# A larger ring of weight tiles in the expert stage: thirteen instead of ten, with the expert inputs kept once in float32 and split tiles of half the size

## The chip, the cores and the metric

The kernel runs on one core of a Trainium2 chip. The metric is the device time of one execution in microseconds (us); three executions of the kernel before give a median of 1507.25 us (1500.32 to 1512.21).

## The reference, cut to what matters

A two-layer transformer trunk, one sequence of 256 tokens, width 1024, all in float32. Everything up to the last feed-forward block stands in the same order in both kernels. The block that the change is about is the mixture of experts at the end:

```python
def moe_swiglu(u, w_router, wg, wu, wd):            # u: 256 tokens x 1024
    logits = (xf @ w_router).astype(F32)            # 8 experts
    vals, idx = lax.top_k(logits, TOP_K_EXPERTS)    # 2 of them for each token
    w = jax.nn.softmax(vals, axis=-1)
    gate = jnp.sum(jax.nn.one_hot(idx, N_EXPERTS, dtype=F32) * w[..., None], axis=1)
    for e in range(N_EXPERTS):                      # wg, wu: 1024 x 3584, wd: 3584 x 1024
        y = y + gate[:, e:e + 1].astype(xf.dtype) * swiglu(xf, wg[e], wu[e], wd[e])
```

`u` is the normalized and modulated residual, and `swiglu(u, wg, wu, wd)` is `(silu(u @ wg) * (u @ wu)) @ wd`. The weights of the eight experts are 352 MB in float32, and each is read once.

## The kernel before, in words

**Experts by load.** A router ranks the experts by the number of tokens they got. The four fullest are "heavy" and get 128 token slots, the other four are "light" and get 64 (`SLOTS`). They are worked in turns, heavy, light, heavy, light (`ORDER`). A pair is one heavy and one light expert.

**Two ways to multiply.** For a heavy expert every weight is split into a high and a low float32r part, and each product is three matmuls: high by high, low by high, high by low (`mm3`, L379 to L382). ScalarE (ACT) writes the high part (a cast, L319), VectorE (DVE) subtracts it from the weight (L323). When the split has to be held back, it goes through L321 and L325, which add a zero made from what is waited for (`hold`, `wait`). For a light expert TensorE (PE) reads the raw float32 weights without a split (L1242, L1340); two 64-column halves of the array run at a time, and one float32 matmul of the source is two instructions on PE.

**Stages of an expert.** The hidden width of 3584 is taken in two parts, `CHS` = 2048 and 1536 columns ("first part", "second part"). For each part: the gate matrix in 8 tiles (`chunks_up`), then the silu of the result on ACT (`gated_of`, L1414/L1416), then half of the down matrix of the part before (`chunks_down`, `half(0)`), then the up matrix in 8 tiles, then the product of the two on DVE (`hidden_of`, L1426/L1428), then the other half of the down matrix of the part before (`half(1)`). So after the first part of a heavy expert's gate or up matrix come down tiles of the light expert before it (none for the first expert), and after its second part come its own down tiles.

**The gather.** `pick` builds a 0/1 matrix `P` (tokens by slots) and multiplies the normalized tokens with it on PE (L1188). The tokens are kept as `xh` (high part) and `xl` (low part), both float32r, 2 tiles of 128 x 1024 each. `low()` computes `xl` on DVE (L1050) after the router's choice; the first held splits wait for it.

**The ring.** Weights land in tiles of 128 x 2048 float32 (8 KB a partition, 1 MB). The first 13 tiles of the expert stage come from a list `once`; after it, `ring` hands out ten buffers in turn (eight of pool `raw`, two of `raw2`). SyncE (SP) issues all loads in order (L1215 for gate and up, L1320 for down), each when its buffer's last reader is done.

**The split tiles.** Pool `hl` has four `wh` and four `wl` tiles of 128 x 1024 each. `run` keeps up to three pieces of work prepared ahead of the one that PE uses (`AHEAD = 2`): for a heavy expert a piece is 1024 columns (six matmuls; 512 columns at the end of the second part), for a light one a whole tile.

```python
AHEAD = 2
...
while ready <= AHEAD:
    item = next(work, None)
    ...
    prepare, use = item
    queue.append((use, prepare and prepare(), prepare is not None))
    ready += prepare is not None
```

A scheduler in the tile framework sets the order of instructions on each engine; each engine runs its own list in order.

## Time and profile before

| | us |
|---|---|
| median of 3 executions | 1507.25 |
| lowest, highest | 1500.32, 1512.21 |
| the profiled execution | 1512.12 |
| its span, first to last instruction | 1509.8 |

The profile was taken from one execution. A line such as L323 is a line of the kernel before. "Busy" is the time in which an engine had an instruction running; instructions of one engine overlap at their ends, so a step from one start to the next is shorter than a duration. PEclk is the clock that the chip granted to TensorE, 1.00 being 2.4 GHz and 0.50 being 1.2 GHz. "Idle before" names the time for which an engine stood still and what ended that.

### The profile page before, as it was taken

How to read it: one execution, taken by the hardware profiler on the slowest of the kernel's cores; microseconds unless marked ns; L12 is line 12 of the kernel's file. 1: busy time of each engine (PE TensorE's matmuls, PEld its weight loads, DVE VectorE, ACT ScalarE, POOL GpSimd, SP SyncE). 2: the span in 40 equal slices, each digit the busy share in tenths (PEclk: the TensorE clock that was granted, in tenths of full speed). 3: DMA queues.
4: the chain of work that ended last, by engine and by line, in shares of the span. 5: the costliest groups of instructions: out<-in, count | busy, mean ns of one | idle time of the engine just before them, and what ended most of it. 6: DMA issues, size and time to landing. Idle time of an engine off the chain costs nothing. (4 is left out here: it accounts for less than half of the span.)

```text
span 1509.8 us, 19315 instructions
## 1 busy us (share of the span) xinstructions
PE 1436.0 (95%) x6845; PEld 945.7 (63%) x6845; DVE 940.2 (62%) x1552; ACT 704.5 (47%) x1102; POOL 6.3 (0%) x31
## 2 busy tenths in 40 slices
PE   6999899999999998999999999999999999999995
PEld 3764678888677547788554767445767445676541
DVE  3875599887778654899342778433677334686412
ACT  3536443434444554777223656323665314574311
POOL 0000000000000000000000000000000000000000
PEclk9999999999999969899999999999999999999998
DMA  9846679995767004669999999999999999999995
GB/s 340 325 156 230 257 277 364 365 332 198 243 231 260 40 1 168 209 241 381 405 369 396 421 405 403 368 408 408 420 374 411 367 401 420 419 362 422 391 419 217
DMA packets 118093, 484.01 MB, mean 321 GB/s; under 512 B 10410, under 2 KB 20836, under 8 KB 87268
## 3 DMA queue, kind: packets, MB, share of 16 engines
q1 hardware_dynamic: 117616, 482.60, 82.9%
q8 instruction: 56, 0.92, 0.2%
q14 instruction: 49, 0.40, 0.1%
q10 hardware_dynamic: 372, 0.10, 0.0%
HBM read 481.61 MB, written 1.05 MB: 320 GB/s over the span
## 5 line engine op out<-in xcount | busy, mean ns | idle before, releaser
L323 DVE TENSOR_TENSOR wl<-raw,wh 128x1024 fp32r<-128x1024 f32 (+1 forms) x468 | 515.2, 1138 | 114.3 <-ACT wh L319 105.2
L319 ACT CAST wh<-raw 128x1024 fp32r<-128x1024 f32 (+2 forms) x477 | 455.3, 985 | 267.3 <-PE mm L381 166.2
L1242 PE MATMUL mm<-raw,xr 128*64 128x512 f32 (+1 forms) x1024 | 206.3, 545 | 0.0
L380 PE MATMUL mm<-wh,e 128*128 128x512 f32 x448 | 178.5, 399 | 2.9 <-ACT wh L319 2.9
L381 PE MATMUL mm<-wh,e 128*128 128x512 f32 x448 | 177.2, 396 | 0.0
L380 PE MATMUL mm<-wh,uh 128*128 128x512 f32 (+4 forms) x432 | 163.5, 382 | 4.0 <-ACT wh L319 3.3
L381 PE MATMUL mm<-wh,ul 128*128 128x512 f32 (+4 forms) x432 | 163.6, 379 | 2.2 <-DVE ul L345 2.2
L382 PE MATMUL mm<-wl,uh 128*128 128x512 f32 (+4 forms) x432 | 160.9, 377 | 2.3 <-DVE wl L325 2.0
L382 PE MATMUL mm<-wl,e 128*128 128x512 f32 x448 | 151.4, 401 | 0.0
L1242 PEld LDWEIGHTS mm<-raw,xr 128*64 128x64 f32 x1024 | 68.2, 136 | 110.7 <-issue 102.1
L1340 PE MATMUL y<-raw,lh 128*64 128x512 f32 x448 | 108.6, 599 | 3.3 <-DMA raw<-in_moe_w_down 2.2
L380 PEld LDWEIGHTS mm<-wh,e 128*128 128x128 f32 x448 | 85.5, 191 | 23.8 <-ACT wh L319 6.1
L382 PEld LDWEIGHTS mm<-wl,e 128*128 128x128 f32 x448 | 84.7, 191 | 24.7 <-DVE wl L323 2.7
L381 PEld LDWEIGHTS mm<-wh,e 128*128 128x128 f32 x448 | 85.3, 190 | 17.4
L380 PEld LDWEIGHTS mm<-wh,uh 128*128 128x128 f32 x432 | 83.1, 194 | 20.3 <-ACT wh L319 4.4
L381 PEld LDWEIGHTS mm<-wh,ul 128*128 128x128 f32 x432 | 83.2, 193 | 19.2 <-DVE ul L345 3.8
L382 PEld LDWEIGHTS mm<-wl,uh 128*128 128x128 f32 x432 | 82.4, 192 | 16.5 <-DVE wl L325 2.4
L380 PE MATMUL y<-wh,th 128*128 128x512 f32 x224 | 90.2, 403 | 2.4 <-ACT wh L319 2.4
L381 PE MATMUL y<-wh,tl 128*128 128x512 f32 x224 | 89.2, 398 | 0.0
L382 PE MATMUL y<-wl,th 128*128 128x512 f32 x224 | 79.8, 403 | 1.0 <-DVE wl L323 0.7
L1340 PEld LDWEIGHTS y<-raw,lh 128*64 128x64 f32 x448 | 30.9, 136 | 61.9 <-issue 53.1
L1305 ACT COPY lh<-tp 128x512 f32<-128x512 f32 (+1 forms) x16 | 8.1, 533 | 114.2 <-PE y L1340 75.9
(366 smaller groups left out, 1610.1 us busy)
## 6 DMA issues: line engine op xcount, KB each, us to landing
raw<-in_moe_w_down SPq DMA_DIRECT2D x112, 1024.0 KB, 8.8
raw<-in_moe_w_gate SPq DMA_DIRECT2D x64, 1024.0 KB, 11.1
raw<-in_moe_w_up SPq DMA_DIRECT2D x62, 1024.0 KB, 8.4
raw<-in_moe_w_gate SPq DMA_DIRECT2D x64, 768.0 KB, 9.0
raw<-in_moe_w_up SPq DMA_DIRECT2D x64, 768.0 KB, 6.5
raw<-in_w_ada SPq DMA_DIRECT2D x37, 1024.0 KB, 7.3
raw<-in_ffn_w_gate SPq DMA_DIRECT2D x10, 1024.0 KB, 8.5
raw<-in_ffn_w_up SPq DMA_DIRECT2D x9, 1024.0 KB, 8.6
```

Of the source, the lines that this page charges most:

```text
L319: S.copy(hi, src)
L323: V.tensor_tensor(lo, src, hi.bitcast(F32), op=ALU.subtract)
L380: T.matmul(dst, xh, wh, start=start, stop=False)
L381: T.matmul(dst, xl, wh, start=False, stop=False)
L382: T.matmul(dst, xh, wl, start=False, stop=stop)
L1242: T.matmul(box[q // 512][64 * i:64 * i + 64, 0:qn], x[:, k], w_[:, i * hf + q:i * hf + q + qn], start=(k == 0), stop=(k == 7))
L1305: S.copy(ht[0][:, bs], pv)
L1340: T.matmul(py[r][0][64 * nn:64 * nn + 64], tt[0][:, b, 64 * i:64 * i + 64], w_[:, jj, cs], start=a, stop=z)
```

## The change

The normalized tokens are kept once, as plain float32 (`xh`); `xl`, `low()` and the wait for them go, and the gather multiplies in float32. The split tiles become one tile of 128 x 1024 for each 512 columns, high part in its first half and low part in its second; there are four of them (names `wh` and `wl` in turn, two buffers each), and a piece of heavy work is 512 columns (three matmuls). In the earlier stages two pools of two buffers stand for one of four, the second of them in the rooms that are given back before the expert stage. The room that this frees (24 KB a partition) makes three more weight tiles: a third buffer in `raw2`, and a new pool `raw4` of two on the left side of the memory, where the rooms of the earlier stages were. The list `once` has 16 tiles, the ring 13 buffers.

```diff
-    hlp = ctx.enter_context(tc.tile_pool(name="hl", bufs=4))
+    hlp = ctx.enter_context(tc.tile_pool(name="hl", bufs=2))
...
+    hls = [hlp, phA.enter_context(tc.tile_pool(name="hl2", bufs=2))]
...
-            wh = hlp.tile([128, HLW], F32R, name="wh")
-            wl = hlp.tile([128, HLW], F32R, name="wl")
+            hls.append(hls.pop(0))
+            wh, wl = (hls[0].tile([128, HLW], F32R, name=x) for x in ("wh", "wl"))
...
-    raw2 = ctx.enter_context(tc.tile_pool(name="raw2", bufs=2, side="right"))
+    raw2 = ctx.enter_context(tc.tile_pool(name="raw2", bufs=3, side="right"))
...
-    xh = mq.tile([128, NT, D], F32R, name="xh")
-    xl = mq.tile([128, NT, D], F32R, name="xl")
+    xh = mq.tile([128, NT, D], F32, name="xh")
...
-    def low():
-        for t in range(NT):
-            r = rs[:, t:t + 1]
-            if t == 1:
-                r = mq.tile([128, 1], F32, name="rs2")
-                V.tensor_scalar(r, rs[:, t:t + 1], zero_of(rk[:, 1, 0:1]), None, op0=ALU.add)
-            V.scalar_tensor_tensor(xl[:, t], h[:, t], r, xh[:, t].bitcast(F32), op0=ALU.mult, op1=ALU.subtract)
-        hold((first, None), *[(zero_of(xl[:, 1, 0:1]), first)] * 3)
+    hold((first, None), *[(zero_of(rk[:, 1, 0:1]), first)] * 7)
...
+    raw4 = ctx.enter_context(tc.tile_pool(name="raw4", bufs=2))
...
-    once[:] = [main] * 2 + [lambda: raw3.tile([128, 2048], F32, name="raw")] + [main] * 6 + [wide] * 2 \
-        + [lambda: xrp.tile([128, 2048], F32, name="xr"), lambda: latep.tile([128, 2048], F32, name="late")]
-    ring[:] = [main] * 8 + [wide] * 2
+    more = lambda: raw4.tile([128, 2048], F32, name="raw")
+    once[:] = [main] * 2 + [lambda: raw3.tile([128, 2048], F32, name="raw")] + [main] * 6 + [wide] * 3 \
+        + [lambda: xrp.tile([128, 2048], F32, name="xr"), lambda: latep.tile([128, 2048], F32, name="late")] + [more] * 2
+    ring[:] = [main] * 8 + [wide] * 3 + [more] * 2
...
-        P = mp.tile([128, NT, 256], F32R, name="P", bufs=2)
+        P = mp.tile([128, NT, 256], F32, name="P", bufs=2)
...
-                n = 0
-                for xx in (xh, xl):
-                    for t in range(NT):
-                        T.matmul(p[:, i * 256 + a:i * 256 + z], xx[:, t, k * 128:(k + 1) * 128], P[:, t, a:z],
-                                 start=(n == 0), stop=(n == 3))
-                        n += 1
+                for t in range(NT):
+                    T.matmul(p[:, i * 256 + a:i * 256 + z], xh[:, t, k * 128:(k + 1) * 128], P[:, t, a:z],
+                             start=(t == 0), stop=(t == 1))
...
+    half_of = ["wl", "wh"]
+
+    def split_512(src):
+        half_of.append(half_of.pop(0))
+        w = hlp.tile([128, HLW], F32R, name=half_of[0])
+        split(w[:, 0:512], w[:, 512:1024], src, *(wait.pop(0) if wait else ()))
+        return w[:, 0:512], w[:, 512:1024]
...
-                    cn = min(HLW, n - c)
-                    wh = hlp.tile([128, HLW], F32R, name="wh")[:, 0:cn]
-                    wl = hlp.tile([128, HLW], F32R, name="wl")[:, 0:cn]
-                    split(wh, wl, raw[0][:, c:c + cn], *(wait.pop(0) if wait else ()))
-                    return wh, wl
+                    return split_512(raw[0][:, c:c + 512])
...
-            for c in range(0, n if heavy else 1, HLW):
+            for c in range(0, n if heavy else 1, 512):
...
-            for j in range(2 if heavy else 1):
-                yield (lambda j=j, prepare=prepare: prepare(j)), (lambda w_, j=j, use=use: use(j, w_))
+            for j, nn in ((0, 0), (0, 1), (1, 0), (1, 1)) if heavy else ((0, 0),):
+                yield (lambda j=j, nn=nn, prepare=prepare: prepare(j, nn)), (lambda w_, j=j, nn=nn, use=use: use(j, nn, w_))
...
-        next(steps)
-        if first:
-            low()
```

How it moves instructions, at three places. First, PE at the start of the expert stage, from the end of the router's ranks (L1028) to the first products of expert 0; `tp` are the gather's results, `mm` the sums of the gate matrix, `e` the gathered input. Before:

```order
L1028 MATMUL tp_5263<-sel_5017,onesF_96 128x8
L1188 MATMUL tp_5287<-P_5275,xh_5008 128x128
L1188 MATMUL tp_5304<-P_5275,xh_5008 128x128
L1188 MATMUL tp_5287<-P_5275,xh_5008 128x128
L1188 MATMUL tp_5287<-P_5275,xl_5009 128x128
L1188 MATMUL tp_5304<-P_5275,xh_5008 128x128
L1188 MATMUL tp_5304<-P_5275,xl_5009 128x128
L1188 MATMUL tp_5287<-P_5275,xl_5009 128x128
```

The same place in the kernel of the change:

```order
L1028 MATMUL tp_5265<-sel_5019,onesF_99 128x8
L1181 MATMUL tp_5287<-P_5283,xh_5011 128x128
L1181 MATMUL tp_5300<-P_5283,xh_5011 128x128
L1181 MATMUL tp_5287<-P_5283,xh_5011 128x128 x3
L1181 MATMUL tp_5300<-P_5283,xh_5011 128x128 x3
L381 MATMUL mm_5405<-wh_5396,e_5286 128x512
```

The matmuls with `xl` are gone, half as many remain, and they are in float32.

Second, ACT at the end of the second part of expert 0's gate matrix (`gated_of`): the casts of its own down tiles (`raw_5997` before, `raw_6048` now), a copy for the down input (`th`), and the three silus. Before:

```order
L319 CAST wh_5999<-raw_5997 128x1024
L319 CAST wh_6009<-raw_5997 128x1024
L319 CAST wh_6025<-raw_6023 128x1024
L319 CAST wh_6043<-raw_6023 128x1024
L1305 CAST th_5844<-tp_6016 128x512
L319 CAST wh_6055<-raw_6053 128x1024
L1416 ACTIVATE sg_6031<-mm_5846,hold_6029 128x512
L1416 ACTIVATE sg_6031<-mm_5847,hold_6029 128x512
L1416 ACTIVATE sg_6031<-mm_5848,hold_6029 128x512
L319 CAST wh_6065<-raw_6053 128x1024
```

Now:

```order
L320 CAST wh_6050<-raw_6048 128x512
L320 CAST wl_6056<-raw_6048 128x512
L320 CAST wh_6069<-raw_6048 128x512
L320 CAST wl_6083<-raw_6048 128x512
L1299 CAST th_5879<-tp_6062 128x512
L1403 ACTIVATE sg_6074<-mm_5881,hold_6072 128x512
L1403 ACTIVATE sg_6074<-mm_5882,hold_6072 128x512
L1403 ACTIVATE sg_6074<-mm_5883,hold_6072 128x512
L320 CAST wh_6091<-raw_6089 128x512
```

The silus stand behind four pieces of 512 columns instead of five of 1024.

Third, DVE at the end of the second part of expert 0's up matrix (`hidden_of`): low parts of its own down tiles, and the three products `sg`; `xr` are gathered inputs of the light expert. Before:

```order
L323 TENSOR_TENSOR wl_6258<-raw_6255,wh_6257 128x1024
L323 TENSOR_TENSOR wl_6268<-raw_6255,wh_6267 128x1024
L323 TENSOR_TENSOR wl_6277<-raw_6274,wh_6276 128x1024
L149 TENSOR_SCALAR hold_6280<-wl_6268 128x1
L1203 TENSOR_SCALAR xr_5806<-tp_6285,Af1_907,Bf1_908 128x64
L1428 SCALAR_TENSOR_TENSOR sg_6031<-sg_6031,hold_6280,mm_6125 128x512
L1428 SCALAR_TENSOR_TENSOR sg_6031<-sg_6031,hold_6280,mm_6126 128x512
L1428 SCALAR_TENSOR_TENSOR sg_6031<-sg_6031,hold_6280,mm_6127 128x512
```

Now (`wh` and `wl` are both whole split tiles here):

```order
L324 TENSOR_TENSOR wh_6332<-raw_6330,wh_6332 128x512
L324 TENSOR_TENSOR wl_6338<-raw_6330,wl_6338 128x512
L324 TENSOR_TENSOR wh_6344<-raw_6330,wh_6344 128x512
L150 TENSOR_SCALAR hold_6347<-wl_6338 128x1
L1195 TENSOR_SCALAR xr_5849<-tp_6359,Af1_910,Bf1_911 128x64
L1415 SCALAR_TENSOR_TENSOR sg_6074<-sg_6074,hold_6347,mm_6184 128x512
L1415 SCALAR_TENSOR_TENSOR sg_6074<-sg_6074,hold_6347,mm_6185 128x512
L1415 SCALAR_TENSOR_TENSOR sg_6074<-sg_6074,hold_6347,mm_6186 128x512
L1195 TENSOR_SCALAR xr_5849<-tp_6359,Af1_910,Bf1_911 128x64
```

The products stand behind three pieces in both; a piece has half the columns now. On SP the loads stand in the same order in both kernels, but for one load of `raw2` that moves ahead of the tile `late`.

## Rows read from the trace of the kernel before

**Rows 1.** The page: busy time and its share of the span by engine; then the busy share of the DMA engines in tenths, in 40 equal slices of the span.

```profile
PE 1436.0 (95%) x6845; PEld 945.7 (63%) x6845; DVE 940.2 (62%) x1552; ACT 704.5 (47%) x1102; POOL 6.3 (0%) x31
...
DMA  9846679995767004669999999999999999999995
```

**Rows 2.** Busy time of each engine in stretches of the expert stage: start and end, length, PE, PEld, DVE, ACT, POOL busy (number of instructions), PEclk, DMA share, GB/s. Two of the four pairs of experts.

```profile
823.00:1043.00 220.00, 214.06 (x974) 131.63 (x974) 126.64 (x154) 103.12 (x132) 0.00 (x0) 1.00 1.00 402
1043.00:1265.00 222.00, 215.53 (x974) 132.89 (x974) 126.47 (x150) 103.94 (x132) 0.00 (x0) 0.99 0.99 398
```

**Rows 3.** What PE waited for from 613 to 1492 us: waiting engine, tile and line, what ended the wait, us in total, times, longest.

```profile
PE tp L421 <- DVE tl L1307: 4.6, 3, 1.5
PE mm L380 <- ACT wh L319: 2.9, 3, 1.0
...
PE y L1340 <- DMA raw<-in_moe_w_down: 2.2, 3, 1.3
...
PE y L1340 <- SPq L1486: 0.4, 1, 0.4
```

**Rows 4.** The last tiles of the last light expert, PE in order of time: start, length, engine, line, operation, tiles, form, count, idle time before and what ended it.

```profile
1482.11 1.94 PE L1340 MATMUL y<-raw,lh 128*64 128x512 f32 x8 [0.55 <-DMA raw<-in_moe_w_down]
1484.38 1.94 PE L1340 MATMUL y<-raw,lh 128*64 128x512 f32 x8 [0.33 <-DMA raw<-in_moe_w_down]
1487.60 1.94 PE L1340 MATMUL y<-raw,lh 128*64 128x512 f32 x8 [1.28 <-DMA raw<-in_moe_w_down]
```

**Rows 5.** PE in order of time in the gather between two tiles of a light expert.

```profile
755.26 1.94 PE L1242 MATMUL mm<-raw,xr 128*64 128x512 f32 x8
757.13 0.47 PE L1188 MATMUL tp<-P,xl 128*128 128x192 f32 x2
757.43 0.39 PE L1188 MATMUL tp<-P,xh 128*128 128x192 f32 x2
757.75 1.94 PE L1242 MATMUL mm<-raw,xr 128*64 128x512 f32 x8
```

**Rows 6.** DVE in order of time at the start of the expert stage.

```profile
604.40 0.15 DVE L149 TENSOR_SCALAR hold<-rk 128x1 int32<-128x1 int32 x1
604.58 0.21 DVE L1049 TENSOR_SCALAR rs<-rsr,hold 128x1 f32<-128x1 f32 x1
604.90 1.28 DVE L1050 SCALAR_TENSOR_TENSOR xl<-h,rs,xh 128x1024 fp32r<-128x1024 f32 x1
606.22 0.15 DVE L149 TENSOR_SCALAR hold<-xl 128x1 int32<-128x1 int32 x1
606.48 2.48 DVE L325 SCALAR_TENSOR_TENSOR wl<-raw,hold,wh 128x1024 fp32r<-128x1024 f32 x2
```

**Rows 7.** Groups by line and shape, from 600 us on: busy us in all, mean ns of one, idle time before and what ended it.

```profile
L323 DVE TENSOR_TENSOR wl<-raw,wh 128x1024 fp32r<-128x1024 f32 x296 | 352.4, 1223 | 85.9 <-ACT wh L319 78.5
L319 ACT CAST wh<-raw 128x1024 fp32r<-128x1024 f32 x296 | 303.4, 1053 | 112.6 <-PE mm L381 55.0 <-PE y L381 29.4 <-DMA raw<-in_moe_w_down 25.6
...
L323 DVE TENSOR_TENSOR wl<-raw,wh 128x512 fp32r<-128x512 f32 x64 | 44.1, 688 | 0.0
...
L319 ACT CAST wh<-raw 128x512 fp32r<-128x512 f32 x64 | 39.6, 618 | 2.5 <-PE y L381 1.7 <-PE mm L381 0.6
```

**Rows 8.** PE in order of time just ahead of the expert stage, three-matmul products back to back.

```profile
591.77 0.39 PE L382 MATMUL mm<-wl,uh 128*128 128x512 f32 x1
592.00 0.39 PE L380 MATMUL mm<-wh,uh 128*128 128x512 f32 x1
...
593.81 0.39 PE L382 MATMUL mm<-wl,uh 128*128 128x512 f32 x1
```

**Rows 9.** ACT in order of time: casts without a pause; the four silus behind the first part of expert 0's gate matrix; the three behind the second part of a later heavy expert's.

```profile
620.29 3.93 ACT L319 CAST wh<-raw 128x1024 fp32r<-128x1024 f32 x4
...
636.84 2.42 ACT L1416 ACTIVATE sg<-mm,hold 128x512 f32<-128x512 f32 x4
...
902.50 1.84 ACT L1416 ACTIVATE sg<-mm,hold 128x512 f32<-128x512 f32 x3 [0.68 <-DVE hold L149]
```

**Rows 10.** DVE in order of time: splits without a pause, then the products behind the second part of a later heavy expert's up matrix, and two subtractions of 512 columns in a row.

```profile
627.37 8.03 DVE L323 TENSOR_TENSOR wl<-raw,wh 128x1024 fp32r<-128x1024 f32 x7
...
930.02 0.75 DVE L1428 SCALAR_TENSOR_TENSOR sg<-sg,hold,mm 128x512 f32<-128x512 f32 x1
930.69 1.22 DVE L323 TENSOR_TENSOR wl<-raw,wh 128x1024 fp32r<-128x1024 f32 x1
931.82 1.40 DVE L1428 SCALAR_TENSOR_TENSOR sg<-sg,hold,mm 128x512 f32<-128x512 f32 x2
933.14 5.76 DVE L323 TENSOR_TENSOR wl<-raw,wh 128x1024 fp32r<-128x1024 f32 x5
942.36 1.29 DVE L1307 TENSOR_TENSOR tl<-tp,th 128x512 fp32r<-128x512 f32 x2 [3.46 <-ACT th L1305]
```

**Rows 11.** Stretches as in rows 2: four stretches of one heavy expert or more.

```profile
650.00:700.00 50.00, 50.00 (x234) 41.22 (x233) 46.60 (x59) 38.03 (x48) 0.00 (x0) 1.00 0.85 308
700.00:1475.00 775.00, 755.38 (x3450) 457.21 (x3450) 422.97 (x513) 343.25 (x433) 0.00 (x0) 0.99 0.99 400
1044.00:1048.00 4.00, 4.00 (x12) 3.08 (x11) 4.00 (x4) 3.66 (x5) 0.00 (x0) 0.57 1.02 420
1048.00:1060.00 12.00, 12.00 (x54) 9.94 (x53) 11.19 (x11) 9.13 (x9) 0.00 (x0) 1.00 1.01 419
```

More of the change, by code (lines that the diff above doesn't have):

```diff
@@ L1234, in use @@
                 if heavy:
-                    for q in range(0, min(HLW, n - c), 512):
-                        cs = slice(q, q + 512)
-                        mm3(box[(c + q) // 512], x[0][:, k], x[1][:, k], w_[0][:, cs], w_[1][:, cs], k == 0, k == 7)
+                    mm3(box[c // 512], x[0][:, k], x[1][:, k], w_[0], w_[1], k == 0, k == 7)
                 else:
@@ L1243, in use @@
                                      w_[:, i * hf + q:i * hf + q + qn], start=(k == 0), stop=(k == 7))
-                if c + HLW >= (n if heavy else 0) and k % 2 and between:
+                if c + 512 >= (n if heavy else 0) and k % 2 and between:
                     between.pop(0)()
-            for c in range(0, n if heavy else 1, HLW):
+            for c in range(0, n if heavy else 1, 512):
                 yield (lambda c=c, prepare=prepare: prepare(c)), (lambda w_, c=c, use=use: use(c, w_))
@@ L1275, in slots @@
         for t in range(NT):
-            T.transpose(p[:, t * 128:(t + 1) * 128], P[:, t].bitcast(F32), identF)
+            T.transpose(p[:, t * 128:(t + 1) * 128], P[:, t], identF)
         S.copy(PT, p[:, 0:256].rearrange("p (t q) -> p t q", t=NT))
@@ L1279, in slots @@
         for t in range(NT):
-            T.matmul(p[:, 0:1], P[:, t].bitcast(F32), gateS[:, t, r:r + 1], start=(t == 0), stop=(t == 1))
+            T.matmul(p[:, 0:1], P[:, t], gateS[:, t, r:r + 1], start=(t == 0), stop=(t == 1))
         gs = small.tile([128, 1], F32, name="gs", bufs=4)
@@ L1314, in chunks_down, with prepare @@
             raw = []
-            def prepare(j, j0=j0, raw=raw):
-                if j == 0:
+            def prepare(j, nn, j0=j0, raw=raw):
+                if j + nn == 0:
                     src = weights("moe_w_down", r)[c0 + i * n // 2:c0 + (i + 1) * n // 2]
@@ L1322, in prepare, with use @@
                     return raw[0]
-                wh = hlp.tile([128, HLW], F32R, name="wh")
-                wl = hlp.tile([128, HLW], F32R, name="wl")
-                split(wh, wl, raw[0][:, j], *(wait.pop(0) if wait else ()))
-                return wh, wl
-            def use(j, w_, j0=j0):
+                return split_512(raw[0][:, j, nn * 512:(nn + 1) * 512])
+            def use(j, nn, w_, j0=j0):
                 tt = ht[r, c0, n]
-                if c0 + i + j0 + j == 0:
+                if c0 + i + j0 + j + nn == 0:
                     py[r] = [ps_y() for _ in range(SLOTS[r] // 64)]
@@ L1334, in use @@
                     a, z = c0 + i + b == 0, c0 + n == DFFE and i == 1 and b == NB - 1
+                    if heavy:
+                        mm3(py[r][nn], tt[0][:, i * NB + b], tt[1][:, i * NB + b], *w_, a, z)
+                        continue
                     for nn in range(2):
-                        cs = slice(nn * 512, (nn + 1) * 512)
-                        if heavy:
-                            mm3(py[r][nn], tt[0][:, i * NB + b], tt[1][:, i * NB + b], w_[0][:, cs], w_[1][:, cs], a, z)
-                        else:
-                            T.matmul(py[r][0][64 * nn:64 * nn + 64], tt[0][:, b, 64 * i:64 * i + 64], w_[:, jj, cs],
-                                     start=a, stop=z)
-            for j in range(2 if heavy else 1):
-                yield (lambda j=j, prepare=prepare: prepare(j)), (lambda w_, j=j, use=use: use(j, w_))
+                        T.matmul(py[r][0][64 * nn:64 * nn + 64], tt[0][:, b, 64 * i:64 * i + 64],
+                                 w_[:, jj, nn * 512:(nn + 1) * 512], start=a, stop=z)
+            for j, nn in ((0, 0), (0, 1), (1, 0), (1, 1)) if heavy else ((0, 0),):
+                yield (lambda j=j, nn=nn, prepare=prepare: prepare(j, nn)), (lambda w_, j=j, nn=nn, use=use: use(j, nn, w_))
     def back(r, py, PT, gs, last):
```

## The prediction

> **What bounds the kernel now.** I read the page first. PE is busy in 95% of the span, and the DMA engines too stand at 9 tenths in nearly every slice of the second half [rows 1]: either could be the bound. The stretches tell more: in a pair of experts PE is busy for 214.06 of 220.00 and 215.53 of 222.00 us at a clock of 1.00, while the DMA share is 1.00 and 0.99 [rows 2]. So both are full, and only the waits say which one waits for the other. In the whole expert stage, 879 us long, PE waited on a weight tile at one place only, in the light expert's down matrix: 2.2 us in three waits, and 0.4 for SP [rows 3]. In order of time the larger of these lie in the last ten microseconds of the stage, 0.55, 0.33 and 1.28 [rows 4]: there the ring no longer helps, since the loads end when they end. Everywhere else PE's waits are short and end on ACT or DVE [rows 3]. PE is the bound, the loads run at its pace, and the reader should see that a DMA share of 1.00 does not say that anything waits for DMA.
>
> **The gather in float32.** Only the gathers of three pairs (192 slots) lie between tiles that PE has at hand, 8 slices each: 24 groups. Now one group is four float32r matmuls; from 757.13 to the next tile at 757.75 it takes 0.62 us [rows 5]. Afterwards it is two float32 products, four instructions. The light tile ahead of it has eight float32 instructions of 512 columns, two at a time side by side, in 755.26 to 757.13 = 1.87, so 0.47 for one; by columns 0.47 x 192 / 512 = 0.175. Four are 0.70, so +0.08 x 24 = **+2.0**. Bounds: 0, if they flow as the four do now, and +7, if each takes a full float32r step of 0.227 (4 x 0.227 - 0.62 = 0.29, x 24). The gathers of 128 and 64 slots wait for other things, and I cost them at nothing; if that cover is gone, 16 more groups of at most 0.1 add 1.6.
>
> **The start.** The first held splits wait for `xl`, whose second tile is written from 604.90 on and whose zero stands at 606.22; the zero made from `rk` stands at 604.40 [rows 6]. With `low()` gone the splits could start 606.22 - 604.40 = 1.8 earlier, and the first piece has half the columns (L325: 2.48 for two of 1024 [rows 6], so some 0.6 less for 512). What is late next is the gather, with its `P` and the copy of its result. I take **-1.5**, bounds -3.3 and 0. The stage ahead of it loses nothing to two pools of two buffers: they hand out the same four.
>
> **The splits.** A subtraction of 1024 columns takes 1.223 us on DVE and one of 512 takes 0.688; the casts take 1.053 and 0.618 on ACT [rows 7]. That is 304 more instructions on each engine. PE's step is (593.81 - 591.77) / 9 = 0.227 [rows 8]: three matmuls 0.68, six 1.36. Instructions overlap: seven subtractions of 1024 without a pause take 8.03, a step of 1.135, and four casts 3.93 [rows 9, 10]. For 512 columns the two subtractions (L307) in a row, 1.29 for both, make a step of about 0.60 if the second ends 0.69 after its start [rows 7, 10]. So per 1024 columns DVE needs 2 x 0.60 = 1.20 instead of 1.135 of PE's 1.36: slower, but still covered. Where cover can go is after a burst of other work on ACT or DVE, since four buffers now hold half as many columns.
>
> I count from PE's start on a piece, and allow 0.16 for the signal between engines (no row shows it alone). Afterwards: the buffer comes free at 0.68 + 0.16 = 0.84, is cast at 1.46, split at 2.15; PE wants the high part at 4 x 0.68 = 2.72 and the low part two matmuls later, 3.17. ACT can be held up by 2.72 - 1.46 = 1.26, DVE by 3.17 - 2.15 = 1.02. The same for before: free 1.52, cast 2.57, split 3.79, wanted 5.44 and 6.35: 2.87 and 2.56. Now the bursts: the three silus behind the second part of the gate matrix take 1.84 [rows 9]; the three products behind the up matrix 3 x 0.66 (from 931.82 to 933.14 two of them) and an `xr` with its zero, 2.3 in all [rows 10]. Before, both fit. Afterwards PE stands for 1.84 - 1.26 = 0.6 and 2.3 - 1.0 = 1.3, in each of four heavy experts: (0.6 + 1.3) x 4 = 7.6. Behind the first parts, light tiles without a split follow and cover the burst, but not in expert 0, where nothing stands before it: four products and an `xr` are about 3.5, so 2.5 more. Its four silus (2.42 [rows 9]) already made PE wait, 1.0 at most [rows 3], and I add nothing. Two of these waits are long enough for the clock to fall: from 1044 to 1048 it was granted at 0.57, near its lower level of 1.2 GHz, and stood at 1.00 in the next stretch [rows 11]; there 12 matmuls took 4.00 where 12 x 0.227 = 2.7 would do, so 1.3 was lost; for two I take 2.0, since the waits are not all that long. Against it, the first split of a heavy expert is there sooner: 1.053 - 0.618 = 0.43, for three experts 1.3. Sum 7.6 + 2.5 + 2.0 - 1.3 = **+10.8**. Bounds: -3, if the bursts stay hidden and the waits on `wh` (2.9 + 2.4 in all, of which rows 3 shows the first) shrink by half; +33, if no burst finds any slack: (1.84 + 2.3) x 4 + 3.5 = 20, and a dip of 1.3 behind ten of them.
>
> The Trainium skill, Perfetto Trace Analysis, section "Optimizing Scalar/DVE Operations", gives about 60 ns of overhead for a DVE instruction on SBUF; 304 more would be an estimated 18 us, were DVE the bound. The same section says that where neither engine is saturated but they make bubbles elsewhere, smaller instructions can finish work sooner; by that the splits would give back up to 3 us. The rows lie nearer the first in size (1.20 against 1.135, 0.07 a pair) and show neither as a loss on PE.
>
> **Three more tiles in the ring.** PE hardly waits for a tile, so there is little to win: the three waits at the end, and what they let SP be late by, are 2.2 + 0.4 = 2.6 [rows 3]. With thirteen buffers the loads run ahead by three more tiles and end sooner by up to 3 x 2.6 us (1 MB at 400 GB/s [rows 2]): **-2.6**, bounds -4 and 0.
>
> Sum: +2.0 - 1.5 + 10.8 - 2.6 = +8.7. The profiled execution took 1512.1 (its span 1509.8), 4.9 above the median of 1507.25; so 1520.8 for such an execution and **1516** as a median. The bounds of its terms rarely meet: its own range is 1504 to 1530.
>
> **Rivals.** A, faster: the DMA is the bound after all, and deeper loads raise its rate. For it: share 0.99, and 400 GB/s over 700 to 1475 against 420 in the best stretches [rows 11]. Three tiles of 2.5 us (1 MB at 420) gained in each of four pairs would be 7.5 x 4 = 30: 1477. Against it: PE waited 2.6 on loads in all, so nothing more can come back that way unless ACT's and DVE's waits hide some; the places where a tile comes just in time, at the start of a heavy expert, show no DMA wait. The Trainium skill, SBUF — State Buffer, section "A bandwidth-pool intuition that's wrong (but worth ruling out)", holds that what comes from HBM is nearly always the limit end to end; the rows of PE's waits disagree here.
>
> B, slower: DVE becomes the bound in the heavy experts. It decides from the point at which a split of 512 takes longer than three matmuls: 0.688 by its busy time is already over 0.68, 0.60 by the step is not. In 650 to 700 DVE is busy for 46.60 of 50.00 [rows 11]. About 33 splits of 1024 lie in it, 1.223 each, 40; in halves they are 2 x 0.688 x 33 = 45, so DVE would want 51.6 of 50, some 3%. Over 115 us of heavy work per pair, four times, that is 15; the bursts, with no slack to be made up from, 20; dips of the clock 13.5; the gather and the rest 0.5: +49, 1556. Against it: busy times overlap, as the steps show.
>
> C, the change does nothing that it says: the ring is never waited for, and the splits stay covered, because PE's own pauses (gathers, transposes, the light tiles) refill the four buffers before a burst. Then the gather and the start are left, with the few waits at the end: +2.0 - 1.5 and up to +3, about 1510.
>
> **How the numbers follow.** Forecast 0.55, A 0.10, B 0.22, C 0.13. One per cent, 15 us, is about what a measurement of this kernel can tell from no change (the three runs lie 12 apart). Faster by over 1%: A alone, 0.10. Slower by over 1%, above 1522: B, and the upper part of the forecast's own range, 0.13: 0.35. The rest, 0.55, is the same. The range leaves out most of A and the upper half of B, and takes in C: 1496 to 1545.
>
> **What would show it.** In the profile after: PE waits on the ACT cast or the DVE split of 512 right behind the silus and the products of the second parts, of 0.6 and 1.3 us, four times each, and one of about 2.5 in expert 0; PEclk falling at one or two of these. Elsewhere three matmuls still 0.68 apart; if they come at 0.70 or more, with PE waiting on the DVE split throughout and DVE busy without pause, B is right. The gather's group at 0.70 instead of 0.62. The first product of expert 0 some 1.5 earlier than now. No wait on a load in the last ten microseconds. If the span falls by more than 10 us, my view that PE does not wait for the loads is wrong; if no wait stands behind the bursts, the four buffers have more slack than I counted.

## The result, and the profile after

The changed kernel takes 1481.07 us in the median of six runs (1478.97 to 1491.66) against 1507.34 for the kernel before: a ratio of 0.985, 95% interval 0.9821 to 0.9878. The forecast was 1516, range 1496 to 1545: wrong in sign. The profiled executions took 1512.1 before and 1479.0 after, 33 apart, more than the medians. Both kernels' runs lie in three groups 5 to 7 us apart (before near 1500, 1507 and 1512; after near 1480, 1486 and 1492), and the one profiled before is of the slowest: a stretch of half clock in an attention stage, told at the end. Of the 33, 13.8 lie ahead of the gather (it begins at 603.81 before, at 590.03 after), 1.2 between it and the first product, and 18.1 in the stage behind that. So the expert stage is read by itself below.

The page after, against [rows 1]: PE's share is the same, in a shorter span; DVE's and ACT's have risen from 62% and 47%. These are two lines of its parts 1 and 2.

```profile
PE 1407.8 (95%) x6845; PEld 939.5 (64%) x6845; DVE 970.0 (66%) x1852; ACT 756.2 (51%) x1406; POOL 6.3 (0%) x31
...
DMA  9956779996667306569999999999999999999994
```

Stretches after, columns as in [rows 2]: the same two pairs of experts, and 20 us of the attention stage.

```profile
808.00:1025.00 217.00, 211.54 (x974) 134.07 (x974) 135.91 (x230) 116.40 (x209) 0.00 (x0) 0.99 1.00 405
1025.00:1240.50 215.50, 210.01 (x974) 132.85 (x974) 134.77 (x226) 116.26 (x209) 0.00 (x0) 1.00 1.01 409
540.00:560.00 20.00, 19.50 (x112) 11.34 (x109) 10.26 (x37) 13.35 (x39) 0.79 (x3) 1.00 0.01 2
```

The same 974 matmuls of a pair take 217.0 and 215.5 instead of 220.0 and 222.0 of [rows 2], and PE is "busy" in as large a share as before. PE's waits, from the first product on (columns as in [rows 3]), show little of where it comes from: in all, PE stood still for 21.6 us before and 21.0 after, up to the end of the last up matrix. Two rows of before that [rows 3] leaves out, and then rows of after. None of these is on a load.

```profile
PE tp L1188 <- DVE P L1170: 2.6, 1, 2.6
PE y L380 <- ACT wh L319: 2.4, 3, 1.1
```

```profile
PE tp L422 <- DVE tl L1301: 4.6, 3, 1.5
...
PE mm L381 <- ACT wh L320: 2.1, 4, 0.5
PE y L381 <- ACT wh L320: 2.1, 3, 0.7
...
PE tp L1181 <- DVE P L1165: 1.6, 1, 1.6
```

Rows of one size need not be one place: the 2.4 on the cast (`wh`) for a down tile stood behind the gather in light experts, and is gone; the 2.1 after stand behind the silus of heavy ones, and are new.

So I put the two traces side by side in blocks of the same work, each from its first matmul to the next block's first. Sums of the blocks (us):

| block | before | after | |
|---|---|---|---|
| expert 0, first part, both matrices | 53.6 | 57.3 | +3.7 |
| from there to the second heavy expert | 161.3 | 157.3 | -4.0 |
| heavy experts 2 to 4: gate, first part, and the light down tiles behind | 88.8 | 83.7 | -5.1 |
| up, first part, and the light down tiles behind | 96.9 | 91.0 | -5.9 |
| gate, second part, and own down tiles | 85.8 | 88.4 | +2.6 |
| up, second part, and own down tiles | 86.2 | 85.5 | -0.7 |
| light experts 2 to 4: gate, first part | 93.8 | 89.1 | -4.7 |
| the rest of the light experts | 193.0 | 192.6 | -0.4 |
| last down tiles, after the last up matrix | 23.4 | 19.9 | -3.5 |
| stage, first product to last light matmul | 882.9 | 864.8 | -18.1 |

The two losses are in experts where I looked for them. The gains lie in blocks for which I had no term. PE in order of time in the largest of them, the up matrix of a heavy expert, before: the light expert's down tiles behind the up matrix.

```profile
1095.24 1.07 PE L1340 MATMUL y<-raw,lh 128*64 128x512 f32 x2
1096.24 0.73 PE L382 MATMUL mm<-wl,e 128*128 128x512 f32 x2
1096.91 1.93 PE L1340 MATMUL y<-raw,lh 128*64 128x512 f32 x6
1098.77 1.05 PE L421 MATMUL tp<-identF,sg 128*128 128x128 f32 x7
1099.75 1.94 PE L1340 MATMUL y<-raw,lh 128*64 128x512 f32 x8
1101.61 0.38 PE L421 MATMUL tp<-identF,sg 128*128 128x128 f32 x1
1101.92 1.94 PE L1340 MATMUL y<-raw,lh 128*64 128x512 f32 x8
```

And the same place after:

```profile
1074.15 0.39 PE L383 MATMUL mm<-wl,e 128*128 128x512 f32 x1
1074.47 1.94 PE L1330 MATMUL y<-raw,lh 128*64 128x512 f32 x8
1076.34 1.16 PE L422 MATMUL tp<-identF,sg 128*128 128x128 f32 x8
1077.43 3.65 PE L1330 MATMUL y<-raw,lh 128*64 128x512 f32 x16
```

Read starts, not durations. Eight light matmuls in a row take 1.87 (1074.47 to 1076.34), 0.47 for two. Before, the tile at 1095.24 is broken into after two of its eight. These two take 1.00, and the six behind the break 1.86: 0.99 more than eight in a row. That is what would come out if the two halves of the array run their matmuls side by side and the first two, alone, leave one half empty: a pair is broken. The two heavy matmuls that broke in take 0.67 instead of 0.45, and the single transpose at 1101.61 takes 0.31, where eight in a row take 1.09. Nowhere does an idle time stand in the row: PE is busy all the while. After, this tile is whole. The same break, into a pair, stood behind the first part of the gate too, so six times in the heavy experts 2 to 4, and nowhere there after. At 0.99 + 0.22 (0.67 less 0.45) each, that is 7.3 us. The forms say what changes: 128\*64 (two halves of the array) against 128\*128.

The gather goes into fewer gaps as well, against [rows 5]: eight float32 matmuls of 192 columns between two light tiles, instead of four and four in two gaps.

```profile
934.66 1.57 PE L1181 MATMUL tp<-P,xh 128*128 128x192 f32 x8
936.16 1.94 PE L1236 MATMUL mm<-raw,xr 128*64 128x512 f32 x8
938.03 1.57 PE L1181 MATMUL tp<-P,xh 128*128 128x192 f32 x8
```

This gives nothing by itself: the eight take 1.50, two gaps of four took 2 x 0.62 = 1.24. What this block, the light gate, no longer has is a wait behind the gather. Before, PE stood there for the cast of the first down tile of the heavy expert:

```profile
963.29 0.51 PE L1280 MATMUL tp<-gateS,P 128*128 128x1 f32 x4
964.86 0.49 PE L380 MATMUL y<-wh,th 128*128 128x512 f32 x1 [1.06 <-ACT wh L319]
```

The 36 matmuls from 964.86 on took 9.4, after 8.5: with the 1.06 some 2 us, in each of two light experts. In "splitonly" and in "f32only" below this wait is gone too, so either part of the change removes it.

The Trainium skill, TensorEngine Tiling (Array Packing), section "Key Properties", says that changing the tiling mode drains the engine. The trace agrees in so far as the lone transpose and the two heavy matmuls cost more between light tiles; the price is measured below, and a drain as such stands in no row. It is a rule that bore on this change, and I had not weighed it.

I counted in every trace how often a light matmul is followed by anything else on PE, from the first product on ("changes"), how many pairs of light matmuls are broken ("pairs"), how many stretches of some 3 us the heavy matmuls ran at 0.43 instead of 0.23 apart ("half clock"), and three times of the stage:

| kernel | ring | changes | pairs | half clock | first product to end of last up matrix | last down tiles | both |
|---|---|---|---|---|---|---|---|
| before | 10 | 88 | 6 | 4 | 859.5 | 23.4 | 882.9 |
| after | 13 | 63 | 1 | 2 | 844.9 | 19.9 | 864.8 |
| again | 13 | 63 | 1 | 2 | 845.1 | 19.9 | 865.0 |
| ring10 | 10 | 67 | 1 | 1 | 844.7 | 25.1 | 869.8 |
| splitonly | 10 | 78 | 1 | 4 | 850.3 | 23.9 | 874.2 |
| f32only | 10 | 83 | 7 | 2 | 853.3 | 23.9 | 877.2 |
| null_light | 13 | 139 | 1 | 3 | 894.5 | 19.9 | 914.4 |
| null_heavy | 13 | 62 | 1 | 2 | 873.1 | 19.9 | 893.0 |
| six | 12 | 61 | 0 | 5 | 855.3 | 20.2 | 875.5 |
| six_tiles | 12 | 64 | 0 | 2 | 843.3 | 19.9 | 863.2 |
| apart_all | 13 | 56 | 1 | 2 | 840.8 | 19.9 | 860.7 |
| nohold | 13 | 63 | 1 | 2 | 848.9 | 19.9 | 868.8 |
| best | 13 | 56 | 1 | 0 | 836.0 | 19.9 | 855.9 |

### The profile page after: what moved, and what is told of

It reads as the page before. It is cut to its first block, busy times and chain, and to the rows that moved or that the text cites. A ratio compares the mean times of both kernels' runs of the same rounds, so it can differ in the third digit from the quotient of the medians.

```text
span 1476.9 us, 19667 instructions
## 1 busy us (share of the span) xinstructions
PE 1407.8 (95%) x6845; PEld 939.5 (64%) x6845; DVE 970.0 (66%) x1852; ACT 756.2 (51%) x1406; POOL 6.3 (0%) x31
## 5 line engine op out<-in xcount | busy, mean ns | idle before, releaser
L320 ACT CAST wh<-raw 128x512 fp32r<-128x512 f32 (+4 forms) x445 | 321.9, 724 | 251.4 <-PE mm L382 113.9
L324 DVE TENSOR_TENSOR wh<-raw,wh 128x512 fp32r<-128x512 f32 x328 | 225.8, 689 | 61.8 <-ACT wh L320 58.9
L324 DVE TENSOR_TENSOR wl<-raw,wl 128x512 fp32r<-128x512 f32 x328 | 225.3, 687 | 2.1 <-ACT wl L320 1.2
L320 ACT CAST wl<-raw 128x512 fp32r<-128x512 f32 x328 | 203.8, 621 | 22.2 <-PE mm L383 11.5
L324 DVE TENSOR_TENSOR wl<-raw,wh 128x1024 fp32r<-128x1024 f32 (+3 forms) x108 | 125.5, 1170 | 28.0 <-ACT wh L320 25.9
L1330 PE MATMUL y<-raw,lh 128*64 128x512 f32 x448 | 99.9, 596 | 0.7 <-ACT lh L1299 0.7
L381 PE MATMUL mm<-wh,e 128*128 128x512 f32 x224 | 90.4, 403 | 2.5 <-ACT wh L320 2.1
L383 PE MATMUL mm<-wh,e 128*128 128x512 f32 x224 | 89.1, 398 | 0.0
L381 PE MATMUL mm<-wl,e 128*128 128x512 f32 x224 | 88.8, 397 | 0.3 <-ACT wl L320 0.2
L383 PE MATMUL mm<-wl,e 128*128 128x512 f32 x224 | 88.4, 395 | 0.2 <-DVE wl L324 0.2
L382 PE MATMUL mm<-wh,e 128*128 128x512 f32 x224 | 88.1, 393 | 0.0
L382 PE MATMUL mm<-wl,e 128*128 128x512 f32 x224 | 88.0, 393 | 0.0
```

What stands on the lines that cost most here:

```text
L320: S.copy(hi, src)
L324: V.tensor_tensor(lo, src, hi.bitcast(F32), op=ALU.subtract)
L381: T.matmul(dst, xh, wh, start=start, stop=False)
L382: T.matmul(dst, xl, wh, start=False, stop=False)
L383: T.matmul(dst, xh, wl, start=False, stop=stop)
L1330: T.matmul(py[r][0][64 * nn:64 * nn + 64], tt[0][:, b, 64 * i:64 * i + 64], w_[:, jj, nn * 512:(nn + 1) * 512], start=a, stop=z)
```

## The experiments

Two theories stood against each other. R: the loads held PE back although no wait names them, and the larger ring gives the gain. O: the gain comes from the order of PE's instructions.

**The changed kernel again.** No edit.

> The changed kernel once more, beside its parts. In its first profile the expert stage, from the first product of expert 0 to the last of PE, took 867 us where the kernel before took 885, and PE named hardly any wait on a load in either. Both theories: about 1480, 26 below the kernel before; the stage at 866 to 869. Some 10 us of the difference between the two profiles lay in an attention stage (520 to 560 us) that the change does not touch, where the kernel before ran at a granted clock of 0.70: if this belongs to the execution and not to the kernel, it comes and goes in both.

1480.10, ratio 0.9837 (0.98 to 0.9874), the stage 865.0: the blocks repeat within 0.2 us but for the place of a half-clock stretch.

**The ring alone taken back.**

```diff
-    raw2 = ctx.enter_context(tc.tile_pool(name="raw2", bufs=3, side="right"))
+    raw2 = ctx.enter_context(tc.tile_pool(name="raw2", bufs=2, side="right"))
-    raw4 = ctx.enter_context(tc.tile_pool(name="raw4", bufs=2))
-    ring[:] = [main] * 8 + [wide] * 3 + [more] * 2
+    ring[:] = [main] * 8 + [wide] * 2
```

> The changed kernel with ten tiles in the ring instead of thirteen and thirteen loads ahead instead of sixteen, all else as changed; the order of PE stays nearly the same. Theory R (the loads held PE back although no wait names them, and the larger ring gives the gain): back to the kernel before or worse, 1500 to 1515, the stage at 880 or more. Theory O (the gain comes from the order of PE's instructions, which the smaller split pieces and the float32 gather change: fewer transposes and gathers between light tiles): it keeps all but the waits on loads at the very end, about 3.5, so 1484, the stage at 871.

1487.62 (0.9869, 0.9838 to 0.9899). Up to the end of the last up matrix it is the changed kernel to 0.2 us, 844.7, with four changes more and one half-clock stretch fewer, which come to about the same. All that the three tiles give is in the last down tiles, 25.1 against 19.9, and there PE waits on loads again, as this row of its waits shows (changed: none):

```profile
PE y L1328 <- DMA raw<-in_moe_w_down: 3.1, 6, 0.8
```

Theory R falls: it asked for 880. The ring is worth 5.2 us, at the end only.

**The split tiles alone; the gather alone.** Each is one part of the diff on the kernel before.

```diff
+                    return split_512(raw[0][:, c:c + 512])
```

> The kernel before with the split pieces of 512 columns in four tiles alone: the gather stays in two float32r parts, the ring at ten. Theory R: no gain, 1505 to 1520 (the smaller buffers can only cost). Theory O: the transposes move from between light tiles to heavy work (70 changes from a light tile to a transpose become 48), worth some 4 us, and about as much in the changes between heavy and light work: 1498, the stage at 877.

1491.33 (0.9906, 0.9875 to 0.9936).

```diff
-    xh = mq.tile([128, NT, D], F32R, name="xh")
-    xl = mq.tile([128, NT, D], F32R, name="xl")
+    xh = mq.tile([128, NT, D], F32, name="xh")
```

> The kernel before with the gather in float32 alone: no low part of the tokens, pieces of 1024 columns and a ring of ten as before. Theory R: 1506, the gather itself costing up to 2 and the start giving 1.5. Theory O: half as many changes between light tiles and the gather (44 to 26 from light to gather), worth 3 to 4 us, and an earlier start of the first product by 1 to 2: 1502, the stage at 881.

1492.70 (0.9907, 0.9879 to 0.9936). The medians hold the attention stage too; by the expert stage, the splits give 8.7 (874.2, theory O said 877) and the gather 5.7 (877.2, O said 881). Together 14.4; with the ring's 5.2 it makes 19.6, against the 18.1 that the change gave. "splitonly" has the blocks "up, first part" at 30.3 each like the changed kernel, "f32only" has them at 32.3 like the one before: there it is the splits that changed the order, and with it the broken pairs. The 5.7 of "f32only" are not its gaps: 13 gaps with the gather alone take 14.9, where 22 took 13.5 before. It has two half-clock stretches fewer, some 3 us, and the wait behind the gather is gone in two light experts, some 4.

**The kernel before, a second look.** No edit.

> The kernel before, a second look with a profile. In its first one (1512) the attention stage from 505 to 560 us ran at a granted clock of 0.59 to 0.87, and took 10 us more than in the five other profiles, whose instructions up to there stand in the same order on every engine. If that belongs to the execution, this look shows a full clock there and 1500 to 1502; if it belongs to the program, the low clock and 1507 or more. The expert stage, first product to last: 888 again by both theories O and R.

1511.74, and the low clock again. The stage repeats: 882.2 against 882.9.

**What a change costs.** 112 small matmuls that add zeros, between light tiles or among heavy pieces.

```diff
+                if not heavy and k < 7:                        # null_light
+                    T.matmul(box[0][:, 0:8], identF, zz, start=False, stop=False)
+                if heavy and k < 7 and c + 512 >= n:           # null_heavy
+                    T.matmul(box[c // 512][:, 0:8], identF, zz, start=False, stop=False)
```

> The changed kernel with 112 more small matmuls (the full array, float32, 8 columns of zeros added to a sum, so the result is the same), each set between two weight tiles of a light expert's gate or up matrix. Theory O (each change from light tiles to anything else costs PE some 0.4 us beside the instruction itself): about 77 of them stand where nothing stood before; 77 x 0.42 and 112 x 0.13 make +47: 1527, and at least 25 more than the twin with the same matmuls among heavy pieces. Rival (an instruction costs PE the same wherever it stands, and the gain of the change lies elsewhere): like the twin, within 5.

1530.17 (1.0175, 1.0133 to 1.0216). 

> The twin: the same 112 small matmuls, each behind the last piece of a heavy expert's weight tile. Theory O: 112 x 0.13, +15: 1495, part of it given back, since the splits win time. Rival: the same as between light tiles.

1508.79 (1.0031, 0.9999 to 1.0063). The light one came out as forecast, the heavy one dearer: by the stage 28.2 / 112 = 0.25 each, not 0.13. So the light ones cost 21.4 more, not 25; the rival said within 5. With 139 - 63 = 76 new changes that is 0.28 for a change; spread over all 112 it would be 0.19, and the two heavy matmuls above show 0.22. So I take 0.2 to 0.3. The neighbours of the twin are float32r, those of the light one float32, so it is not shown that the form of the array alone makes the price. PE in order of time, light tiles with the null matmul, and below heavy pieces:

```profile
769.90 1.51 PE L1236 MATMUL mm<-raw,xr 128*64 128x512 f32 x8
771.34 0.39 PE L1239 MATMUL mm<-zz,identF 128*128 128x8 f32 x2
771.66 1.51 PE L1236 MATMUL mm<-raw,xr 128*64 128x512 f32 x8
```

```profile
700.13 0.39 PE L383 MATMUL mm<-wl,e 128*128 128x512 f32 x1
700.36 0.28 PE L1239 MATMUL mm<-zz,identF 128*128 128x8 f32 x2
700.50 0.48 PE L381 MATMUL mm<-wh,e 128*128 128x512 f32 x1
700.81 0.39 PE L382 MATMUL mm<-wh,e 128*128 128x512 f32 x1
```

Between light tiles it holds PE for 0.32; among heavy ones for 0.14, and the next matmul takes 0.31 instead of 0.23.

**More split tiles.** First six tiles with five pieces ahead; this also left the earlier stages' second pool with one buffer instead of two.

```diff
-    hlp = ctx.enter_context(tc.tile_pool(name="hl", bufs=2))
+    hlp = ctx.enter_context(tc.tile_pool(name="hl", bufs=3))
-    AHEAD = 2
+    AHEAD = 4
```

> The changed kernel with six split tiles of 512 instead of four, five pieces prepared ahead instead of three, and twelve tiles in the ring instead of thirteen. In the changed kernel PE waits about 0.9 behind the silus of each heavy expert's second part, and the first part of expert 0 takes 3.6 more than before. If these are the price of the small buffers: -0.9 x 4 - 2 and +1.6 for the wait on loads at the end that the thirteenth tile hid, about 1476. If the buffers are not what holds it there: no gain, 1481.

1501.36 (0.9973, 0.9953 to 0.9994): a miss. Half of the 20 us was lost ahead of the stage (the gather begins at 599.5 instead of 590.0), where the uneven pools are. In the stage, a wait took the place of the one removed, as PE's waits show:

```profile
PE mm L381 <- DVE sg L1415: 12.2, 3, 4.1
```

Then six tiles, four ahead, the earlier pools as changed:

```diff
+    hl3 = ctx.enter_context(tc.tile_pool(name="hl3", bufs=1))
-    AHEAD = 2
+    AHEAD = 3
```

> Six split tiles as in the run before, but the earlier stages keep their two pools of two and four pieces are prepared ahead instead of five; twelve tiles in the ring. In the run with five ahead PE's wait of 0.85 behind the silus was gone, but the products stood behind five splits on VectorE and PE waited 4 us for them at three places. If the small buffers are the price at the silus: the wait there goes to 0.2 or less, 0.7 x 3 plus some of the 3.6 in expert 0, less up to 1.6 for the twelfth tile: 1478 to 1481. If the order of the products decides: waits for products of 1 us or more at the three places, 1482 to 1486.

1479.45 (0.984, 0.9796 to 0.9884): no gain that can be told. The wait at the silus did not go, it grew: PE stands 1.1 in place of 0.7. ACT in order of time there:

```profile
889.71 0.62 ACT L320 CAST wh<-raw 128x512 fp32r<-128x512 f32 x1 [0.22 <-PE mm L383]
892.25 1.84 ACT L1404 ACTIVATE sg<-mm,hold 128x512 f32<-128x512 f32 x3 [1.92 <-DVE hold L150]
893.97 0.62 ACT L320 CAST wl<-raw 128x512 fp32r<-128x512 f32 x1
```

The silus are held until DVE has done a piece ahead, and DVE now has more pieces to do first: ACT stands idle for 1.92 with the silus in front of it.

**Fewer changes.** The way back of a heavy expert is put off to the next heavy one.

```diff
-            (deferred if SLOTS[r] == 64 else between).extend([...])
+            (deferred if SLOTS[r] == 64 else deferred2).extend([...])
```

> The changed kernel with one piece of work moved: the way back of a heavy expert's result (matmuls that scatter it to the tokens) is put off to the next heavy expert, instead of standing between the next light expert's tiles. Same instructions, 10 changes fewer from light tiles to something else. Theory O, with a price of 0.28 (the null matmuls, light less heavy) to 0.42 (the rows) a change: 3 to 4 us off the expert stage, 1476 to 1477. Rival (the price is that of the instruction, not of the change): 1480 to 1481, or more, since the work now competes with the splits.

1470.75 (0.9784, 0.974 to 0.9828), the last heavy expert's way back being left out of the computation. The complete one:

```diff
+            (deferred if SLOTS[r] == 64 else between if r == ORDER[-2] else deferred2).extend([...])
```

> As in the run before, but complete: there the way back of the last heavy expert was left out of the computation, here it stands where the changed kernel has it. The same instructions as in the changed kernel, and 8 changes fewer from light tiles to something else. Theory O: 0.28 to 0.42 each, 2.2 to 3.4 off the expert stage, about 1477. Rival (moving it costs the splits as much as it gives the light tiles): 1480 to 1482.

1474.38 (0.9763, 0.9738 to 0.9789); the stage 4.1 shorter with 7 changes fewer. It is a gain with no instruction removed, though 4.1 / 7 = 0.6 is more than the price of a change; what the rest is stays open.

**The hold on the silus.**

```diff
-            zero = zero_after(split_, 0)
+            zero = None
```

> The changed kernel without the zero that holds the silus back until a split piece prepared ahead is done; ScalarE may take them between its casts. If PE's 0.85 behind the silus (three heavy experts) and part of the 3.6 in expert 0 come from the three silus in one go behind four small buffers: 2.5 to 4 off, 1476 to 1478. If the hold is what keeps the casts ahead of the silus: PE waits as long or longer there, 1480 to 1484.

1485.88 (0.9838, 0.9811 to 0.9865), above both forecasts: expert 0's first part takes 53.7 instead of 57.3, the later experts slower by 7.6 together, with PE's waits on the down tiles' cast at 7.3 instead of 2.1:

```profile
PE y L381 <- ACT wh L320: 7.3, 6, 1.2
```

Each forecast was right in one place. So the hold was taken off in expert 0's first part alone:

```diff
+            zero = zero_after(split_, 0) if at_of(key) else None     # not for expert 0's first part
```

> The kernel with the way back of the heavy experts put off (the complete one, 1474), and the silus of expert 0's first part without the zero that holds them back; all other silus keep it. In the run without any hold, expert 0 lost its 3.6 and the later experts got slower by 1 to 3 each, behind waits on the cast. If the hold is what expert 0's heavy part lost: 3 to 3.6 off the stage, 1471. If the waits there come from the small buffers whatever the silus do: 1474.

1471.02 (0.975, 0.9732 to 0.9768), faster than both kernels of the case. ACT in order of time, after and then in this one, at the silus of expert 0's first part:

```profile
622.46 1.28 ACT L1403 ACT_TABLE_LOAD   x1 [0.19 <-DVE hold L150]
623.75 2.42 ACT L1403 ACTIVATE sg<-mm,hold 128x512 f32<-128x512 f32 x4
626.76 0.62 ACT L320 CAST wh<-raw 128x512 fp32r<-128x512 f32 x1 [0.58 <-ACT sg L1403]
```

```profile
621.64 1.28 ACT L1405 ACT_TABLE_LOAD   x1
622.94 0.60 ACT L1405 ACTIVATE sg<-mm 128x512 f32<-128x512 f32 x1
623.43 0.61 ACT L320 CAST wl<-raw 128x512 fp32r<-128x512 f32 x1
623.94 0.62 ACT L320 CAST wh<-raw 128x512 fp32r<-128x512 f32 x1
624.46 1.58 ACT L1405 ACTIVATE sg<-mm 128x512 f32<-128x512 f32 x3
```

A table load and four silus, 3.7 us in one go, stood before the next cast; without the hold two casts come between. What PE saves there (54.1 instead of 57.3) is its wait of 1.6 for `P`, and the half-clock stretch that followed it, some 1.5. It is not what the change had cost: before, the same burst stood there, a wait of 2.6, and a half-clock stretch as well.

## Why the prediction was wrong, point by point

**The bound.** Right: PE is the bound, the loads are not. "ring10" shows it better than the waits could: with ten tiles nothing changes until the last down tiles. Rival A gave 1477, near the time measured, by a mechanism that this run excludes. The sign that I had named for being wrong on it, a span shorter by more than 10 us, came for another reason.

**The three tiles** were put at -2.6 (-4 to 0). They give 3.5 between the profiles and 5.2 in "ring10". Right in place, short in size: I had only the waits of the slower kernel to read. That the same loads are later for a PE that gets through the stage sooner would explain it, and is not shown apart.

**The start** was put at -1.5: from the first gather to the first product 4.6 before (603.81 to 608.44), 3.4 after (590.03 to 593.47), so -1.2.

**The gather** was put at +2.0. Its instructions are dearer, as worked out: eight take 1.50, 0.75 for four where I had 0.70. In "f32only" its own gaps cost 14.9 - 13.5 = 1.4 more: right in sign and near in size, though I took the 24 gaps as given and the scheduler now sets eight in one. What I had no term for is the wait on the cast behind the gather, which went with it, and the half clock.

**The splits** were put at +10.8; alone, they give 8.7 instead. Term by term:
- The allowance of 0.16 for the signal between engines stood in no row. In the trace of before, the cast at 911.47 waits for the matmul that starts at 911.04, and starts 0.20 behind the next one (911.27): near enough.
- The silus of the second parts, 0.6 each: PE stands for 0.69 in three heavy experts, and its step there is 1.08 instead of 0.23, so 0.85 lost; nothing in expert 0 (its block was 30.4 before and after). The place and size are right. The wait is in this row:

```profile
887.30 0.39 PE L383 MATMUL y<-wl,th 128*128 128x512 f32 x1
888.38 0.50 PE L381 MATMUL y<-wh,th 128*128 128x512 f32 x1 [0.69 <-ACT wh L320]
```

- The products of the second parts, 1.3 each: nothing (block -0.7). The products stand where I said, three in 2.06; but eight transposes, just behind them on PE, hold it for 0.97 without needing a split piece:

```profile
914.82 2.06 DVE L1415 SCALAR_TENSOR_TENSOR sg<-sg,hold,mm 128x512 f32<-128x512 f32 x3
916.80 0.68 DVE L324 TENSOR_TENSOR wh<-raw,wh 128x512 fp32r<-128x512 f32 x1
```

```profile
916.58 0.41 PE L382 MATMUL y<-wl,tl 128*128 128x512 f32 x1
916.82 1.21 PE L422 MATMUL tp<-identF,sg 128*128 128x128 f32 x8
917.79 0.48 PE L383 MATMUL y<-wh,th 128*128 128x512 f32 x1
```

- Expert 0's first part, 2.5 by four products on DVE: the block is 3.7 longer, but hardly there. Behind the products PE waits 0.5 for one. The largest piece, 2.8, is in the gate matrix: its 96 products take 26.1 with their waits on casts and splits, at 604 to 613 us, instead of 23.3. With six split tiles and four pieces ahead they take 22.9 ("six_tiles"; there PE waits 3.4 for `P` instead of 1.6), so four small buffers and three pieces are too few at the start of the stage, where I had no burst. Another 2.2 are the steps that make the way back ready (L1270, L1274), with a wait of 0.8: they stand in this block after, in the next one before. So part of the 3.7 has only moved.
- Its four silus, to which I added nothing: I read "1.0 at most" out of [rows 3], and the wait there was 2.6 for `P`, in a row that I left out. After, it is 1.6: PE waits less at this burst, not more.
- The clock, +2.0: two half-clock stretches fewer, not two more, at 1.4 to 1.6 each (the same block with and without one: 30.1 and 28.6 before, 28.95 and 27.4 after). Why they fell away is open.
- The first split of a heavy expert sooner, -1.3: right. PE's wait there (`mm` on the cast) fell from 0.96 to 0.54 at three starts, 1.3 in all.

**The step that failed** is the term of the splits, +10.8, and in it what all the terms have in common. They took PE's instructions to stand where they stood, and priced only what ACT, DVE and the loads would make PE wait. The pieces of 512 columns and the gather of half as many matmuls gave the scheduler other choices: PE broke into the light tiles 63 times instead of 88, and into a pair of light matmuls once instead of six times. Of the 14.6 that were gained ahead of the last down tiles, the broken pairs are 5 x 0.99 = 5.0. Of the 25 changes, 11 are gathers, whose instructions cost about what their changes gave back; the other 14 are 3 to 4 at 0.2 to 0.3. The half clock is 3, and the waits on a cast that fell, behind the gather and at the start of a heavy expert, are 4 and 1.3. These make 16 to 17, and the losses at the silus (2.6) and in expert 0 (some 3) stand against them, so 3 to 4 of the gain are not placed. Both counts were to be had before any run, from the order of PE's instructions in the two programs, and the price of a broken pair from starts in the trace of before. I read the order at three places and not for what breaks into what, and I read PE's waits, in which neither a broken pair nor a change appears, since PE counts as busy.

Of the two rules that I weighed from one section of the Trainium skill (Perfetto Trace Analysis, "Optimizing Scalar/DVE Operations"), the one on overhead would by my estimate from its figure have cost 18, and no run shows that: "splitonly" has as many more instructions and is faster. The other, that breaking up may let work finish sooner, is borne out at five places: 0.96 to 0.54 at three starts and 1.06 to nothing at two. But most of the gain is in PE's order.

## What to carry to other kernels

Where an engine is busy all the time, compare the starts of its instructions block by block: its waits and its busy share were the same in two kernels of which one was 18 us shorter. Before pricing a change of buffers or of piece sizes under a scheduler, count in both orders how often TensorE goes from one tiling of the array to another, and how often it is taken away between two matmuls that would run side by side. A burst on ACT or DVE costs only what is left after whatever PE can do without it, so look what stands on PE at that very place.

## What the runs showed of the hardware that was not expected

- Float32 matmuls on the two halves of the array cost 0.47 for two when eight stand in a row. Two alone take 1.00, and the six behind the break 1.86: a break inside a pair costs 0.99 (six times in the kernel before, once after).
- A change between matmuls on two halves of the array and full ones cost PE 0.19 to 0.28 us beside the instruction (the null matmuls), with no idle time in the trace. A float32 matmul of 8 columns costs 0.25 among full ones of 512.
- The attention stage ran at half clock for some 24 us in three profiles: the stretch 540 to 560 was granted 0.59 in both profiles of the kernel before and 0.61 in "nohold", with 67 matmuls in it where the row of after above has 112:

```profile
540.00:560.00 20.00, 20.00 (x67) 10.17 (x66) 8.43 (x27) 9.83 (x34) 0.00 (x0) 0.61 0.00 1
```

In the other profiles it was granted 1.00. The instructions up to there stand in the same order on PE, ACT and DVE in all the kernels compared ("after", "f32only", "splitonly", "ring10" and "nohold" against the one before), so the order does not decide it; what does is open.
